# A hybrid attention and recurrence block: attention weights times values in plain float32, four gates in the second stage, an early start of the first recurrence head

## The chip, the cores and the metric

The kernel runs on one core of one Trainium2 chip. The core has a matrix engine (TensorE, PE in the profile, with its weight loads as PEld), a vector engine (DVE), a scalar engine (ACT), a general engine (POOL) and a queue that issues transfers (SP). Time is device microseconds of one execution; the number to be predicted is the median of several executions.

## The reference, cut to what matters

1024 frames and 16 learned meta tokens in front of them (1040 rows of 1024 channels) are normalised and projected to 6144 columns. Two branches read the projections: stick-breaking attention with 8 heads of 64, and a gated linear recurrence with 4 heads of 128. Both are gated, projected to 1024 channels, merged by sigmoid gates per channel, and projected once more.

```
proj = u @ w_in            # 1040 x 6144: q k v gate | hq hf hi hgate | gate_sb gate_hg
weights = where(s < t, exp(log_sigmoid(z) + later), 0)      # z = q k^T, later: sum of log(1-beta)
y_sb = (weights @ v) * silu(sb_gate)
S = diag(f) S + (1-f) i^T ;  o = S^T q                      # per recurrence head
y_hg = groupnorm(o) * silu(hg_gate)
merged = sigmoid(gate_sb) * (y_sb @ w_sb_out) + sigmoid(gate_hg) * (y_hg @ w_hg_out)
h = h + merged @ w_out ;  out = rmsnorm(h)
```

All of it is float32. The two gate matrices, gate_sb and gate_hg, have 1024 columns each, that is eight tiles of 128 columns each.

## The kernel before, in words

**Two ways to multiply.** Most products split both operands into a high part that the matrix engine takes in one pass (type F32R) and the rest, and add three products (high by high, high by rest, rest by high). Transposes, and the products inside the recurrence, take plain float32 operands; the trace shows each of these plain products as two records.

**Stages.** (1) Normalise, transpose, first projections. (2) From 67.7 us on, "twins": a projection of 256 columns and all frames is done with seven products of half size in place of eight (`product`, L466; operand preparation in `prep`, L454 on ACT and L455 on POOL). A list `twins` holds eleven of them; the last three are six gate tiles of gate_sb, `N_GS = 6`. Each twin is 7 x 12 matmuls of 512 columns. (3) Attention, from 281 us: four pairs of heads `p`, each with its own projections of v and k. (4) The recurrence, four heads, from 573 us. (5) The projections of the branches, the merge, and the output product.

**What fills the gaps.** Attention and recurrence are chains that pass between engines. Into them a list of projections is threaded: `interleave(steps, lead)` takes for each pair a `main` list of small pieces and a `fill` list, and issues fill pieces in proportion to the main work done, 4 us ahead in attention (LEAD_A) and 2 us in the recurrence (LEAD_B). Fill is the next pair's v and k projections and the gate tiles that are not in a twin: a gate tile there is `gate_group`, 2 halves of 24 matmuls of 512 columns (L259), with a weight fetch of 512 KB, a split of the weights on ACT (L115) and POOL (L120) and a sigmoid on ACT (L1001). `FILL = (2,1,1,1)` says how many gate tiles go into each attention pair, `n = (1,1,2,1)` how many into each recurrence head. What order the instructions then have on each engine is set by the framework's scheduler from this order and its own priorities.

**Attention.** The work of one head comes in units `g = 0..3`, each two blocks of 128 queries. `scores` makes products of queries and keys (L626), a sigmoid on ACT (L628) and a running product along the row on DVE (L631, L635); the result is the sticks `w` (tile `ab`). `values` turns blocks of w by transposes on PE (L668, and L650 for the 16 meta columns), copies them out of PSUM on ACT (L670) as the high part and forms the rest by a subtraction on DVE (L671), then multiplies: the value block with its 64 high and 64 rest columns is the stationary operand, w of two query blocks the moving one,

```
for part in range(2):
    for j in range(2):
        T.matmul(self.av, st["v"][hh][:, 2 * gg + j], wt[:, part, where[j]:where[j] + 256], ...)
```

(L682; four matmuls of 256 columns for each group of up to four blocks, one more for the meta tokens, L685). The sum stands transposed, channels by queries. Its two halves are added (copy on ACT, L688; sum on DVE, L689), and DVE multiplies by the gate (L693). While the values of one unit are made, the scores of the next are threaded between them (`zip_quanta`). PSUM has two buffers for transposes (`tr`), two for scores (`z`), and one for this sum (`av`).

**Recurrence.** `recurrence(hd, ...)` gives twelve pieces. The first, `diagonal`, is DVE work alone (L825 to L843): elementwise products of keys and queries, and the first products of decay factors. `quads` follows with many small matmuls (L852, L858) and DVE updates (L910, L913), then `sixteens` (L877), `halves` (L891), transposes and the state products (L929 to L970). The queries of the head are fetched into a buffer `wt`, of which there are two.

Of the kernel before, what the change touches and what calls it, by code (L numbers as in the profile page):

```python
# [8 lines left out]
F32 = mybir.dt.float32  # L9
F32R = mybir.dt.float32r  # L10
U8 = mybir.dt.uint8
AF = mybir.ActivationFunctionType
# [24 lines left out]
REAL = [(NM, 512), (NM + 512, 512)]  # L37
FULL = [(0, 348), (348, 346), (694, 346)]
QUART = [(0, 256), (256, 256), (512, 256), (768, 272)]
N_GS = 6  # L40
WS = 456
FILL = (2, 1, 1, 1)


@with_exitstack
def block_kernel(ctx: ExitStack, tc: tile.TileContext, x, meta, norm_g, w_in, w_sb_out,
# [379 lines left out]
    twins += [(C_HQ + 2 * P * k, 2 * k, out_silu(kept_hq, HG_SCALE)) for k in range(2)]  # L426
    twins += [(C_HG + 2 * P * k, 2 * k, out_silu(kept_hg, 1.0)) for k in range(2)]
    twins += [(C_GS + 2 * P * k, 2 * k, out_gate(C_GS)) for k in range(N_GS // 2)]

    def ured(c0, t0):  # L430
        return uh[:, c0:c0 + 4, t0:t0 + HT], ul[:, c0:c0 + 4, t0:t0 + HT]
# [73 lines left out]
    here.append(ctx.enter_context(phase("rest")))  # L505


    t = sb("wt", [P, 2, 2, 512], F32R)
    V.memset(t[:, :, :, 0:P].bitcast(F32), 0.0)
    wt_last = [t[:, k] for k in range(2)]  # L510
    t = sb("wt", [P, 2, 2, 512], F32R)
    wt_full = [t[:, k] for k in range(2)]
    n_full = [0]
    t = sb("wtm", [P, 2, 256], F32R)
    V.memset(t.bitcast(F32), 0.0)
    wt_meta = [t[:, k] for k in range(2)]
    t = sb("vm", [P, 2, 2, P], F32R)
    V.memset(t.bitcast(F32), 0.0)
    v_meta = [t[:, k] for k in range(2)]

    later = sb("later", [P, WS])
# [4 lines left out]
    def pair_groups(p):  # L526
        st = {}

        def bk():
            st["k"] = [sb("stk", [P, L], F32R) for _ in range(2)]  # L530
            st["y"] = sb("y", [P, SEQ])
            nc.sync.dma_start(st["y"], kept_sg[p])

        def bv():
            st["vt"] = sb("pt", [P, L + 1])
            st["dv"] = sb("pt", [P, L + 1])
            st["ve"] = sb("ve", [P, NB])
            V.memset(st["vt"][:, 0:1], 0.0)

        def ek(acc, t0, n):  # L540
            for hh in range(2):
                r0, r1 = hh * 64, 64 - hh * 64
                kst = st["k"][hh]
                src = acc[r0:r0 + 64]
                hi = kst[r0:r0 + 64, t0:t0 + n]
                S.activation(hi, src, AF.Copy)
                V.tensor_tensor(kst[r1:r1 + 64, t0:t0 + n], src, hi.bitcast(F32), op=ALU.subtract)

        def ev(acc, t0, n):

            vt = st["vt"]
            S.activation(vt[:, t0 + 1:t0 + n + 1], acc, AF.Copy)
            V.tensor_tensor(st["dv"][:, t0:t0 + n], vt[:, t0:t0 + n], acc, op=ALU.subtract)
            if t0 + n == L:
                G.tensor_copy(st["ve"], vt[:, NM + P:NM + P + (NB - 1) * P + 1:P])

        def v_blocks(b4):
            def emit():
                if b4 == 0:
                    st["v"] = [sb("v", [P, NB, P], F32R) for _ in range(2)]  # L560
                tp = ps("tr").rearrange("p (b n) -> p b n", b=4)
                for b in range(4):
                    t0 = NM + (b4 * 4 + b) * P
                    T.transpose(tp[:, b], st["dv"][:, t0:t0 + P], ident)
                for hh in range(2):
                    src = tp[:, :, hh * 64:hh * 64 + 64]
                    hi = st["v"][hh][:, b4 * 4:b4 * 4 + 4, 0:64]
                    S.activation(hi, src, AF.Copy)
                    V.tensor_tensor(st["v"][hh][:, b4 * 4:b4 * 4 + 4, 64:128], src, hi.bitcast(F32), op=ALU.subtract)
            return (440.0, emit)  # L570

        def v_meta_block():
            vm = v_meta[p % 2]
            st["vm"] = vm
            tp = ps("tr")
            T.transpose(tp[:NM, 0:P], st["dv"][:, 0:NM], ident)
            for r0 in (0, 32):
                src = tp[:NM, 0:P].rearrange("p (h n) -> p h n", h=2)
                S.activation(vm[r0:r0 + NM, :, 0:64], src, AF.Copy)
                V.tensor_tensor(vm[r0:r0 + NM, :, 64:128], src, vm[0:NM, :, 0:64].bitcast(F32), op=ALU.subtract)  # L580

        after_v = [v_blocks(0), v_blocks(1), (110.0, v_meta_block)]
        return st, [proj(C_V + P * p, FULL, ev, bv, after_v), proj(C_K + P * p, FULL, ek, bk)]

# [8 lines left out]
    class Unit:  # L593
# [46 lines left out]
        def values(self):  # L640
# [6 lines left out]
            def meta_t():  # L647
                tp = ps("tr")
                for qi in range(2):
                    T.transpose(tp[:NM, qi * P:(qi + 1) * P], self.w[qi][:, 0:NM], ident)  # L650
                wm = wt_meta[k]
                with tc.high_priority(offset=HP):
                    S.activation(wm[0:NM], tp[:NM, :256], AF.Copy)
                    V.tensor_tensor(wm[32:32 + NM], tp[:NM, :256], wm[0:NM].bitcast(F32), op=ALU.subtract)

            def bank_t(gg):
                def emit():
                    tp = ps("tr")
                    if gg < g:
                        cols = [(j, qi, (j * 2 + qi) * P) for qi in range(2) for j in range(2)]  # L660
                        wt, lo, where = wt_full[n_full[0] % 2], 0, (0, 256)
                        n_full[0] += 1
                    else:
                        cols = [(0, 0, 2 * P), (1, 1, P), (0, 1, 3 * P)]
                        wt, lo, where = wt_last[k], P, (256, 0)
                    for j, qi, c in cols:
                        s0 = NM + (2 * gg + j) * P
                        T.transpose(tp[:, c:c + P], self.w[qi][:, s0:s0 + P], ident)  # L668
                    with tc.high_priority(offset=HP):
                        S.activation(wt[:, 0, lo:], tp[:, lo:], AF.Copy)  # L670
                        V.tensor_tensor(wt[:, 1, lo:], tp[:, lo:], wt[:, 0, lo:].bitcast(F32), op=ALU.subtract)  # L671
                    wts[gg] = (wt, where)
                return (440.0, emit)

            def bank_av(gg):
                def emit():
                    if gg == g:
                        self.av = ps("av")[:, :256]
                    wt, where = wts[gg]
                    for part in range(2):  # L680
                        for j in range(2):
                            T.matmul(self.av, st["v"][hh][:, 2 * gg + j], wt[:, part, where[j]:where[j] + 256],  # L682
                                     start=(gg == g and part == 0 and j == 0), stop=False)
                    if gg == 0:
                        T.matmul(self.av, st["vm"][:, hh], wt_meta[k], start=False, stop=True)  # L685
                        av = self.av
                        tmp = sb("sg", [P, 256])
                        S.activation(tmp[0:64], av[64:128], AF.Copy)  # L688
                        V.tensor_tensor(tmp[r0:r0 + 64], av[0:64], tmp[0:64], op=ALU.add)  # L689
                        for qi in range(2):  # L690
                            b = 2 * g + qi
                            y = st["y"][r0:r0 + 64, P * b:P * (b + 1)]
                            V.scalar_tensor_tensor(y, tmp[r0:r0 + 64, qi * P:(qi + 1) * P], st["ve"][r0:r0 + 64, b:b + 1], y,  # L693
                                                   op0=ALU.add, op1=ALU.mult)
                return (440.0 + 110.0 * (gg == 0), emit)

            q.append(bank_t(g))
            if g > 0:
# [2 lines left out]
            for gg in range(g, -1, -1):  # L701
                q.append(bank_av(gg))
                if gg > 1:
                    q.append(bank_t(gg - 2))
            return q

    def zip_quanta(a, b):

# [381 lines left out]
    late_q = stream(pairs[1][1][:1], pairs[1][1][1])  # L1090
    emit_all(late_q[:CUT])
    emit_all(zip_quanta(late_q[CUT:], both(units[0], "scores")))
    rest = [gate_group(C_GS, e) for e in range(N_GS, 8)] + [gate_group(C_GH, e) for e in range(8)]
    share = FILL
    side, k0 = [], 0
    for p in range(4):
# [6 lines left out]
    for p in range(4):  # L1103
        main = []
        for i in range(6 * p, 6 * p + 6):
            main.append((0.0, lambda i=i: ahead(i + 2)))
            nxt = both(units[i + 1], "scores") if i + 1 < len(units) else []
            main += zip_quanta(both(units[i], "values"), nxt)
            if 7 <= i < 7 + len(MASKS):
                main.append((0.0, lambda h=MASKS[i - 7]: mask_after(h)))  # L1110
        steps.append((main, stream(side[p], side[p + 1][0] if p < 3 else heads[1][1][0])))
    interleave(steps, LEAD_A)

    def hg_gate(h):
# [7 lines left out]

    tail = []
    for h in range(4):
        main, t = recurrence(h, heads[h][0], ("q", "ab", "v", "ab")[h])
        main = main[:2] + tail + main[2:]
        tail = t + [hg_gate(h)]
        n = (1,1,2,1)[h]
        some, rest = rest[:n], rest[n:]
        if h < 3:  # L1130
            fill = stream(heads[h + 1][1] + some, heads[h + 2][1][0] if h < 2 else (rest + sbg)[0])
# [259 lines left out]
```

## Time and profile before

| | |
|---|---|
| median of 3 executions | 892.31 us (892.25 to 893.4) |
| the profiled execution | 892.41 us |
| its span in the profile | 890.7 us, so 1.7 us lie outside it |
| second stage (twins) | 67.7 to 281 us |
| attention, first projections | 281 to 323 us |
| attention, threaded | 323 to 573 us |
| recurrence | 573 to about 740 us |
| busy over the span | PE 868.2, DVE 626.2, ACT 410.9, POOL 280.3 us |

PE rows need care: matmuls overlap in the pipeline, so the mean duration of one is longer than the distance from one to the next. That distance (called pitch below) is read from the chain of waits, where consecutive pieces do not overlap, or from the start times of consecutive rows. Engine shares over the whole span mix stages with different limits.

### The profile page before, as it was taken

What the parts mean: (1) busy time and instruction counts of PE and PEld (TensorE: products, weight loads), DVE (VectorE), ACT (ScalarE), POOL (GpSimd) and SP (SyncE); (2) the same over time, 40 slices, a digit from 0 to 9 for tenths busy, and PEclk for the clock granted to TensorE, in tenths of its full rate; (3) what the DMA queues carried; (4) which work ended last, traced back from release to release, by engine and by line L of the source; (5) the groups of instructions that cost most, each with busy time, mean ns of one, the idle gap of its engine ahead of it and who ended that gap; (6) DMA issues with size and microseconds to landing.
All of it is one profiled execution on the core that took longest, in us unless ns stands there. A gap on an engine that the chain in (4) does not pass through costs nothing.

```text
span 890.7 us, 15024 instructions
## 1 busy us (share of the span) xinstructions
PE 868.2 (97%) x5684; PEld 750.6 (84%) x5684; DVE 626.2 (70%) x1084; ACT 410.9 (46%) x950; POOL 280.3 (31%) x303
## 2 busy tenths in 40 slices
PE   7999999999999999999999999999999999999996
PEld 5998888888888998899899898879788788888885
DVE  6894455645433378789789788867665989998875
ACT  7763334333432455556556556434435364223432
POOL 1027444544451211123211122447261100004551
PEclk9999999999999999999999999999999999999999
DMA  9223444333343512311213212212312357663212
GB/s 286 67 71 93 160 145 131 95 107 118 119 130 116 169 41 67 96 60 48 84 60 96 86 59 60 84 44 102 121 63 80 129 182 259 197 222 125 95 47 96
DMA packets 90587, 98.12 MB, mean 110 GB/s; under 512 B 6017, under 2 KB 65281, under 8 KB 90514
## 3 DMA queue, kind: packets, MB, share of 16 engines
q1 hardware_dynamic: 76832, 73.78, 27.4%
q10 hardware_dynamic: 13682, 23.37, 7.1%
q8 instruction: 45, 0.74, 0.3%
q14 instruction: 28, 0.23, 0.1%
HBM read 71.94 MB, written 25.20 MB: 109 GB/s over the span
## 4 chain that ended last, share of the span: by engine, by line
PE 84%; DVE 8%; ACT 4%; issue 1%; DMA 1%; POOL 0%; ACTq 0%; SPq 0%; DVEq 0%; POOLq 0%
PE acc L259 33%; PE acc L466 10%; PE z L466 7%; PE tr L466 7%; PE acc L1298 4%; PE av L682 3%; PE tr L668 3%; PE z L626 3%; PE z L1298 3%; PE tr L1298 3%; PE acc L350 2%; DVE ab L635 2%; DVE ab L631 1%; ACT sq L169 1%; PE av L949 1%
## 5 line engine op out<-in xcount | busy, mean ns | idle before, releaser
L259 PE MATMUL acc<-uh,wh 128*128 128x346 f32 (+2 forms) x472 | 173.4, 367 | 0.0
L120 POOL TENSOR_TENSOR wl<-wr,wh 128x256 fp32r<-128x256 f32 x92 | 79.0, 879 | 271.8 <-ACT wh L115 244.2
L259 PE MATMUL acc<-ul,wh 128*128 128x346 f32 (+2 forms) x472 | 164.2, 348 | 0.0
L259 PE MATMUL acc<-uh,wl 128*128 128x346 f32 (+2 forms) x472 | 163.8, 347 | 0.0
L259 PEld LDWEIGHTS acc<-uh,wl 128*128 128x128 f32 x472 | 88.8, 188 | 6.8
L259 PEld LDWEIGHTS acc<-uh,wh 128*128 128x128 f32 x472 | 89.0, 189 | 4.2 <-issue 0.4
L259 PEld LDWEIGHTS acc<-ul,wh 128*128 128x128 f32 x472 | 89.2, 189 | 2.9 <-issue 0.4
L455 POOL TENSOR_TENSOR pw<-su,pw 128x512 fp32r<-128x512 f32 x44 | 59.2, 1365 | 42.8 <-ACT pw L454 42.8
L455 POOL TENSOR_TENSOR pw<-wr,pw 128x512 fp32r<-128x512 f32 x33 | 43.7, 1323 | 62.5 <-ACT pw L454 62.5
L628 ACT ACTIVATE ab<-z 128x456 f32<-128x456 f32 (+6 forms) x112 | 49.8, 448 | 26.4 <-PE z L626 25.9
L631 DVE TENSOR_TENSOR_SCAN ab<-ab,later 128x456 f32<-128x456 f32 (+3 forms) x64 | 55.7, 871 | 6.8 <-ACT ab L628 6.1
L466 PE MATMUL acc<-th,pw 128*128 128x512 f32 x176 | 58.0, 390 | 0.0
L671 DVE TENSOR_TENSOR wt<-tr,wt 128x384 fp32r<-128x384 f32 (+1 forms) x80 | 50.4, 630 | 10.0 <-ACT wt L670 7.8
L670 ACT ACTIVATE wt<-tr 128x384 fp32r<-128x384 f32 (+1 forms) x80 | 44.3, 554 | 26.0 <-PE tr L668 25.8
L682 PE MATMUL av<-wt,v 128*128 128x256 f32 x320 | 52.6, 286 | 3.7 <-DVE sg L689 3.1
L626 PE MATMUL z<-stk,q 128*128 128x456 f32 (+6 forms) x224 | 55.8, 331 | 0.0
L454 ACT ACTIVATE pw<-su 128x512 fp32r<-128x512 f32 x44 | 26.0, 626 | 60.9 <-DVE su L449 27.1
L682 PEld LDWEIGHTS av<-wt,v 128*128 128x128 f32 x320 | 46.2, 188 | 8.3 <-DVE sg L689 5.3
L635 DVE TENSOR_TENSOR_SCAN ab<-ab 128x348 f32<-128x348 f32 (+4 forms) x48 | 47.0, 980 | 7.2 <-ACT ab L628 5.7
L668 PE MATMUL tr<-ident,ab 128*128 128x128 f32 x288 | 45.2, 273 | 0.7 <-DVE ab L631 0.7
L115 ACT ACTIVATE wh<-wr 128x256 fp32r<-128x256 f32 x92 | 34.4, 413 | 24.6 <-PE acc L259 15.6
L626 PEld LDWEIGHTS z<-stk,q 128*128 128x128 f32 x224 | 38.3, 189 | 3.4
(378 smaller groups left out, 2035.4 us busy)
## 6 DMA issues: line engine op xcount, KB each, us to landing
wr<-in_w_in SPq DMA_DIRECT2D x48, 512.0 KB, 4.1
q<-q SPq DMA_DIRECT2D x32, 256.0 KB, 4.2
wr<-in_w_out SPq DMA_DIRECT2D x16, 512.0 KB, 3.5
sg<-gate SPq DMA_DIRECT2D x24, 256.0 KB, 3.2
gate<-sg ACTq DMA_DIRECT2D x20, 256.0 KB, 2.0
xb<-in_x SPq DMA_DIRECT2D x7, 512.0 KB, 8.1
gate<-co ACTq DMA_DIRECT2D x12, 256.0 KB, 2.0
pt<-hi SPq DMA_DIRECT2D x4, 520.0 KB, 3.2
```

What stands on the lines that cost most here:

```text
L120: eng.tensor_tensor(lo[:, cs], raw[:, cs], h[:, cs].bitcast(F32), op=ALU.subtract)
L259: T.matmul(acc, a, b, start=(k == 0), stop=(k == total - 1))
L455: G.tensor_tensor(t[:, 1], d[key], t[:, 0].bitcast(F32), op=ALU.subtract)
L466: T.matmul(acc, t[:, part // 2, c], (bh, bl, bh)[part][:, c], start=(c == part == 0), stop=(c == 3 and part == 2))
L626: T.matmul(z, qt[:, k, qo + qi * P:qo + (qi + 1) * P], st["k"][hh][:, c0:c1], start=(k == 0), stop=(k == 1))
L628: S.activation(a[:, c0:c1], z, AF.Sigmoid, scale=-1.0)
L631: ins = V.tensor_tensor_scan(w, w, later[:, WS - (n - c0):][:, ::-1], 1.0, op0=ALU.mult, op1=ALU.max)
L635: V.tensor_tensor_scan(w, w, w, a[:, c1:c1 + 1], op0=ALU.mult, op1=ALU.bypass)
L668: T.transpose(tp[:, c:c + P], self.w[qi][:, s0:s0 + P], ident)
L671: V.tensor_tensor(wt[:, 1, lo:], tp[:, lo:], wt[:, 0, lo:].bitcast(F32), op=ALU.subtract)
L682: T.matmul(self.av, st["v"][hh][:, 2 * gg + j], wt[:, part, where[j]:where[j] + 256], start=(gg == g and part == 0 and j == 0), stop=False)
L1298: T.matmul(a, t[:, part // 2, c], (bh, bl, bh)[part][c][:, n * HT // 2:n * HT // 2 + a.shape[-1]], start=(c == part == 0), stop=(c == 3 an ...
```

## The change

1. **Sticks times values.** The transposed sticks stay one plain float32 tile; no rest is formed on DVE. They are now the stationary operand, one 128x128 block for each matmul, and 64 columns of a plain float32 value tile move. The sum stands queries by channels. One ACT copy puts it into a tile `by_query`, and when both heads of a pair have their columns there, a new piece `close` turns it back with two transposes for each unit (L697 after) and DVE applies the gate out of PSUM (L699 after). `close` of a unit is issued behind the first two pieces of the next one. The value tile is one plain copy.
2. **Gates.** `N_GS = 8`, `N_GH = 2`: two more twins, so four gate tiles leave the fill. `FILL = (0,0,0,2)`, and the recurrence has `n = (0,1,2,1)`.
3. **First head.** The `diagonal` of head 0 stands before the last piece of the last attention unit.
4. **Buffers.** The transposed sticks rotate through four buffers of tag `v`; one of the two `wt` buffers holds `by_query`, the other is free for head 0's queries from the start of attention. Memsets of padded tiles go.

```diff
-N_GS = 6
+N_GS = 8
+N_GH = 2
-FILL = (2, 1, 1, 1)
+FILL = (0, 0, 0, 2)
...
+    twins += [(C_GH + 2 * P * k, 2 * k, out_gate(C_GH)) for k in range(N_GH // 2)]
...
-    t = sb("wt", [P, 2, 2, 512], F32R)
-    V.memset(t[:, :, :, 0:P].bitcast(F32), 0.0)
-    wt_last = [t[:, k] for k in range(2)]
-    t = sb("wt", [P, 2, 2, 512], F32R)
-    wt_full = [t[:, k] for k in range(2)]
+    wt_full = []
+    for _ in range(2):
+        t = sb("v", [P, 2, 512])
+        wt_full += [t[:, k] for k in range(2)]
+    t = sb("wt", [P, 2, NB, P])
+    by_query = [t[:, k] for k in range(2)]
...
                     with tc.high_priority(offset=HP):
-                        S.activation(wt[:, 0, lo:], tp[:, lo:], AF.Copy)
-                        V.tensor_tensor(wt[:, 1, lo:], tp[:, lo:], wt[:, 0, lo:].bitcast(F32), op=ALU.subtract)
-                    wts[gg] = (wt, where)
+                        S.activation(wt[:, :n], tp[:, :n], AF.Copy)
+                    wts[gg] = (wt, cols)
...
-                    for part in range(2):
-                        for j in range(2):
-                            T.matmul(self.av, st["v"][hh][:, 2 * gg + j], wt[:, part, where[j]:where[j] + 256],
-                                     start=(gg == g and part == 0 and j == 0), stop=False)
-                    if gg == 0:
-                        T.matmul(self.av, st["vm"][:, hh], wt_meta[k], start=False, stop=True)
-                        av = self.av
-                        tmp = sb("sg", [P, 256])
-                        S.activation(tmp[0:64], av[64:128], AF.Copy)
-                        V.tensor_tensor(tmp[r0:r0 + 64], av[0:64], tmp[0:64], op=ALU.add)
...
+                    for c, (j, qi) in enumerate(cols):
+                        T.matmul(self.av[:, qi], wt[:, c * P:c * P + P], st["v"][:, 2 * gg + j, r0:r0 + 64],
+                                 start=(gg == g and c == 0), stop=False)
+                    if gg > 0:
+                        return
+                    for qi in range(2):
+                        T.matmul(self.av[:, qi], wt_meta[k][:, qi * P:(qi + 1) * P], st["vm"][:, r0:r0 + 64],
+                                 start=False, stop=(qi == 1))
+                    S.activation(st["o"][:, 2 * g:2 * g + 2, r0:r0 + 64], self.av, AF.Copy)
...
+        def close(self):
+            st, g = self.st, self.g
+            def emit():
+                tp = ps("tr")
+                for qi in range(2):
+                    b = 2 * g + qi
+                    T.transpose(tp[:, qi * P:(qi + 1) * P], st["o"][:, b], ident)
+                    y = st["y"][:, P * b:P * (b + 1)]
+                    V.scalar_tensor_tensor(y, tp[:, qi * P:(qi + 1) * P], st["ve"][:, b:b + 1], y, op0=ALU.add, op1=ALU.mult)
+            return [(220.0, emit)] if self.hh else []
...
-            main += zip_quanta(both(units[i], "values"), nxt)
+            vals = both(units[i], "values")
+            vals[2:2] = both(units[i - 1], "close") if i else []
+            main += zip_quanta(vals, nxt)
+            if i + 1 == len(units):
+                main += both(units[i], "close")
...
+    main0, tail0 = recurrence(0, heads[0][0], "q")
+    last = steps[3][0]
+    for k, quantum in zip((-1,), main0):
+        last.insert(k, quantum)
+    main0 = main0[1:]
...
-        n = (1,1,2,1)[h]
+        n = (0, 1, 2, 1)[h]
```

PE, in the last pair of heads, the values of a unit with g = 3 (tr: a transpose buffer, wt: transposed sticks, v: values, z: scores of the next unit, acc: fill). Before:

```order
L626 MATMUL z_5646<-stk_4645,q_5384 128x328 x2
L682 MATMUL av_5651<-wt_2528,v_4701 128x256 x4
L259 MATMUL acc_5642<-uh_72,wh_5167 128x512
L259 MATMUL acc_5642<-ul_73,wh_5167 128x512
L259 MATMUL acc_5642<-uh_72,wl_5168 128x512
L668 MATMUL tr_5659<-ident_63,ab_5505 128x128 x2
L668 MATMUL tr_5659<-ident_63,ab_5539 128x128 x2
L626 MATMUL z_5667<-stk_4645,q_5384 128x392 x2
L682 MATMUL av_5651<-wt_2530,v_4701 128x256 x4
```

and now, where v_2809 and v_2808 hold the transposed sticks and v_4700 the values:

```order
L620 MATMUL z_5477<-stk_4644,q_5233 128x328 x2
L669 MATMUL av_5482<-v_4700,v_2809 128x64 x3
L260 MATMUL acc_5399<-uh_72,wh_4988 128x512
L260 MATMUL acc_5399<-ul_73,wh_4988 128x512
L260 MATMUL acc_5399<-uh_72,wl_4989 128x512
L656 MATMUL tr_5492<-ident_63,ab_5349 128x128
L656 MATMUL tr_5492<-ident_63,ab_5386 128x128 x2
L656 MATMUL tr_5492<-ident_63,ab_5349 128x128
L260 MATMUL acc_5510<-uh_72,wh_5256 128x512
```

Four matmuls of 256 columns have become three or four of 64; the transposes and the fill around them keep their places.

DVE, where attention ends and head 0 of the recurrence begins. Before:

```order
L689 TENSOR_TENSOR sg_5833<-av_5823,sg_5833 64x256
L693 SCALAR_TENSOR_TENSOR y_4646<-sg_5833,ve_4394,y_4646 64x128 x2
L689 TENSOR_TENSOR sg_5844<-av_5838,sg_5844 64x256
L693 SCALAR_TENSOR_TENSOR y_4646<-sg_5844,ve_4394,y_4646 64x128 x2
L825 TENSOR_TENSOR ab_5849<-stk_5160,wt_5163 128x1024
L915 TENSOR_TENSOR ab_5853<-stk_5159 128x520
L827 TENSOR_TENSOR wt_5163<-wt_5163,stk_5159 128x1024
```

and now:

```order
L625 SCALAR_TENSOR_TENSOR ab_5606<-ab_5606,later_2813 128x144
L625 SCALAR_TENSOR_TENSOR ab_5606<-ab_5606,later_2813 128x272
L820 TENSOR_TENSOR ab_5718<-stk_4981,wt_4984 128x1024
L910 TENSOR_TENSOR ab_5722<-stk_4980 128x520
L822 TENSOR_TENSOR wt_4984<-wt_4984,stk_4980 128x1024
L910 TENSOR_TENSOR ab_5722<-ab_5722 128x260
L836 TENSOR_TENSOR wt_4984<-wt_4984,stk_4980 128x256x2
```

The diagonal (L825, now L820) stood behind the last gate products of attention; it now stands directly behind the last running products, ahead of the gate products of the last three units (L699).

PE at the same place, now (before, the first L852 stood 19 rows behind the last L685):

```order
L674 MATMUL av_5689<-vm_2812,wtm_2811 128x64 x2
L847 MATMUL z_5730<-ab_5718,o_684_4233 32x256 x4
L853 MATMUL z_5735<-wt_4984,stk_4981 32x48 x21
L669 MATMUL av_5706<-v_4700,v_2809 128x64 x3
L674 MATMUL av_5706<-vm_2812,wtm_2811 128x64 x2
L697 MATMUL tr_5713<-ident_63,wt_2810 128x128
```

The first small products of the recurrence (L847, L853) now stand between the products of the last two units, ahead of the last of them.

More of the change, by code (lines that the diff above doesn't have):

```diff
@@ L505, in block_kernel @@
     here.append(ctx.enter_context(phase("rest")))
-    t = sb("wt", [P, 2, 2, 512], F32R)
-    V.memset(t[:, :, :, 0:P].bitcast(F32), 0.0)
-    wt_last = [t[:, k] for k in range(2)]
-    t = sb("wt", [P, 2, 2, 512], F32R)
-    wt_full = [t[:, k] for k in range(2)]
+    wt_full = []
+    for _ in range(2):
+        t = sb("v", [P, 2, 512])
+        wt_full += [t[:, k] for k in range(2)]
     n_full = [0]
-    t = sb("wtm", [P, 2, 256], F32R)
-    V.memset(t.bitcast(F32), 0.0)
+    t = sb("wt", [P, 2, NB, P])
+    by_query = [t[:, k] for k in range(2)]
+    t = sb("wtm", [NM, 2, 256])
     wt_meta = [t[:, k] for k in range(2)]
-    t = sb("vm", [P, 2, 2, P], F32R)
-    V.memset(t.bitcast(F32), 0.0)
+    t = sb("vm", [NM, 2, P])
     v_meta = [t[:, k] for k in range(2)]
@@ L559, in emit @@
                 if b4 == 0:
-                    st["v"] = [sb("v", [P, NB, P], F32R) for _ in range(2)]
+                    st["v"] = sb("v", [P, NB, P])
                 tp = ps("tr").rearrange("p (b n) -> p b n", b=4)
@@ L564, in emit @@
                     T.transpose(tp[:, b], st["dv"][:, t0:t0 + P], ident)
[L565 to L569, printed above, removed]
+                S.activation(st["v"][:, b4 * 4:b4 * 4 + 4], tp, AF.Copy)
             return (440.0, emit)
         def v_meta_block():
-            vm = v_meta[p % 2]
-            st["vm"] = vm
+            st["vm"] = v_meta[p % 2]
             tp = ps("tr")
             T.transpose(tp[:NM, 0:P], st["dv"][:, 0:NM], ident)
[L577 to L580, printed above, removed]
+            S.activation(st["vm"], tp[:NM, 0:P], AF.Copy)
+        st["o"] = by_query[p % 2]
         after_v = [v_blocks(0), v_blocks(1), (110.0, v_meta_block)]
@@ L650, in meta_t @@
                     T.transpose(tp[:NM, qi * P:(qi + 1) * P], self.w[qi][:, 0:NM], ident)
-                wm = wt_meta[k]
                 with tc.high_priority(offset=HP):
-                    S.activation(wm[0:NM], tp[:NM, :256], AF.Copy)
-                    V.tensor_tensor(wm[32:32 + NM], tp[:NM, :256], wm[0:NM].bitcast(F32), op=ALU.subtract)
+                    S.activation(wt_meta[k], tp[:NM, :256], AF.Copy)
             def bank_t(gg):
@@ L658, in emit @@
                     tp = ps("tr")
[L659 to L666, printed above, removed]
+                    cols = [(0, 0), (0, 1), (1, 1)] + [(1, 0)] * (gg < g)
+                    wt = wt_full[n_full[0] % 4]
+                    n_full[0] += 1
+                    for c, (j, qi) in enumerate(cols):
                         s0 = NM + (2 * gg + j) * P
-                        T.transpose(tp[:, c:c + P], self.w[qi][:, s0:s0 + P], ident)
+                        T.transpose(tp[:, c * P:c * P + P], self.w[qi][:, s0:s0 + P], ident)
+                    n = len(cols) * P
                     with tc.high_priority(offset=HP):
-                        S.activation(wt[:, 0, lo:], tp[:, lo:], AF.Copy)
-                        V.tensor_tensor(wt[:, 1, lo:], tp[:, lo:], wt[:, 0, lo:].bitcast(F32), op=ALU.subtract)
-                    wts[gg] = (wt, where)
+                        S.activation(wt[:, :n], tp[:, :n], AF.Copy)
+                    wts[gg] = (wt, cols)
                 return (440.0, emit)
@@ L677, in emit @@
                     if gg == g:
-                        self.av = ps("av")[:, :256]
-                    wt, where = wts[gg]
-                    for part in range(2):
-                        for j in range(2):
-                            T.matmul(self.av, st["v"][hh][:, 2 * gg + j], wt[:, part, where[j]:where[j] + 256],
-                                     start=(gg == g and part == 0 and j == 0), stop=False)
-                    if gg == 0:
-                        T.matmul(self.av, st["vm"][:, hh], wt_meta[k], start=False, stop=True)
-                        av = self.av
-                        tmp = sb("sg", [P, 256])
[L688 to L695, printed above, removed]
+                        self.av = ps("av")[:, :P].rearrange("p (q n) -> p q n", q=2)
+                    wt, cols = wts[gg]
+                    for c, (j, qi) in enumerate(cols):
+                        T.matmul(self.av[:, qi], wt[:, c * P:c * P + P], st["v"][:, 2 * gg + j, r0:r0 + 64],
[6 more added lines that the diff above has]
+                    S.activation(st["o"][:, 2 * g:2 * g + 2, r0:r0 + 64], self.av, AF.Copy)
+                return (440.0 + 220.0 * (gg == 0), emit)
             q.append(bank_t(g))
@@ L1092, in block_kernel @@
     emit_all(zip_quanta(late_q[CUT:], both(units[0], "scores")))
-    rest = [gate_group(C_GS, e) for e in range(N_GS, 8)] + [gate_group(C_GH, e) for e in range(8)]
+    rest = [gate_group(C_GS, e) for e in range(N_GS, 8)] + [gate_group(C_GH, e) for e in range(N_GH, 8)]
     share = FILL
@@ L1124, in block_kernel @@
     for h in range(4):
-        main, t = recurrence(h, heads[h][0], ("q", "ab", "v", "ab")[h])
+        main, t = recurrence(h, heads[h][0], (None, "ab", "v", "ab")[h]) if h else (main0, tail0)
         main = main[:2] + tail + main[2:]
         tail = t + [hg_gate(h)]
-        n = (1,1,2,1)[h]
+        n = (0, 1, 2, 1)[h]
         some, rest = rest[:n], rest[n:]
```

## The prediction

> **What bounds the kernel now.** I read the page first, then busy time by stage, then the chain of waits for the distances between instructions, then the waits.
>
> ```profile
> span 890.7 us, 15024 instructions
> PE 868.2 (97%) x5684; PEld 750.6 (84%) x5684; DVE 626.2 (70%) x1084; ACT 410.9 (46%) x950; POOL 280.3 (31%) x303
> PE 84%; DVE 8%; ACT 4%; issue 1%; DMA 1%; POOL 0%; ACTq 0%; SPq 0%; DVEq 0%; POOLq 0%
> ```
>
> PE is busy for 97% and holds 84% of the chain that ended last. By stage (start:end, length, busy time of each engine):
>
> ```profile
> 67.70:281.00 213.30, 213.30 (x931) 174.35 (x931) 101.79 (x149) 78.00 (x137) 103.28 (x80) 1.00 0.38 121
> 323.00:390.00 67.00, 66.34 (x425) 59.70 (x424) 53.55 (x90) 37.72 (x90) 12.00 (x12) 1.00 0.25 76
> 520.00:573.00 53.00, 51.43 (x346) 46.22 (x345) 44.15 (x79) 31.38 (x76) 11.07 (x12) 1.00 0.21 61
> 323.00:573.00 250.00, 245.20 (x1618) 224.53 (x1617) 205.17 (x353) 143.79 (x350) 53.48 (x73) 1.00 0.24 72
> 573.00:612.00 39.00, 37.90 (x513) 32.30 (x512) 28.82 (x55) 14.91 (x48) 20.50 (x18) 1.00 0.29 95
> ```
>
> The columns behind the length are PE, PEld, DVE, ACT, POOL. In the second stage PE never rests. In threaded attention it is idle for 250 - 245.2 = 4.8 us, in head 0 of the recurrence for 1.1 us. So PE time taken out anywhere after 67.7 us shortens the kernel nearly one for one, as long as the other engines keep up; DVE is the next, 205 of 250 us in attention and 83% (44.15 of 53) in its last quarter, which has least fill and most idle PE (1.57 us).
>
> **The gates.** The chain gives the pitch of both kinds of projection:
>
> ```profile
> 757.93 42.08 PE acc L259 x180
> 84.39 5.55 PE acc L466 x24
> 103.71 5.55 PE acc L466 x24
> ```
>
> 42.08/180 = 0.2338 us for a 512-column matmul; a gate tile in the fill is 48 of them, 11.2 us, four are 44.9 us. The same place of one twin and the next is 103.71 - 84.39 = 19.32 us apart, so two more twins cost 38.6 us. Out of attention go three tiles (five, now two), out of the recurrence one (five, now four). PE: 38.6 - 44.9 = **-6.2 us**. The twins' operand preparation on POOL fills 103 of 213 us and stays covered by PE; without that cover two twins would cost 18.8 us of POOL work, less than their 38.6.
>
> **Sticks times values on PE.** The old form and the nearest plain float32 rows:
>
> ```profile
> 567.08 0.47 PE av L682 x4
> L682 PE MATMUL av<-wt,v 128*128 128x256 f32 x320 | 52.6, 286 | 3.7 <-DVE sg L689 3.1 <-DVE wt L671 0.3
> L685 PE MATMUL av<-wtm,vm 128*128 128x256 f32 x32 | 9.1, 284 | 0.0
> L668 PE MATMUL tr<-ident,ab 128*128 128x128 f32 x288 | 45.2, 273 | 0.7 <-DVE ab L631 0.7
> 602.13 0.94 PE av L949 x8
> 617.97 0.44 PE tr L991 x4
> 43.70 0.66 PE L189 MATMUL tr<-ident,xb 16*128 16x16 f32 x8
> 594.82 0.61 PE z L891 x16
> ```
>
> Before: 0.47/4 = 0.1175 us, times 320 + 32, is 41.4 us. After: 288 blocks (as many as transposes, L668) and 32 x 2 meta products, each plain, so two records each as in L949 and L891: 704 records. No row has 128 weight columns and 64 moving ones. L949 moves 128 columns in at most 0.94/8 = 0.118 us a record; by the L991 pitch, 0.11, half of it is 0.055, the lower end. L189 loads 128 weight columns of 16 rows and moves 16: 0.66/8 = 0.083 with the pipeline's tail, and with a tail of about 0.2 us taken off (an estimate from L682's mean of 286 against its pitch of 118) near 0.062. L891 loads 64 columns of all 128 rows and moves 64: two records make 128 weight columns in 2 x 0.61/16 = 0.076, which I take as the upper end. I choose 0.062: the row that has the same number of weight columns. 704 x 0.062 = 43.6, so **+2.3 us** (from -2.7 to +12.1).
>
> A rule speaks against this. The Trainium skill, TensorE: Matmul & The Clock Gate, section "LDWEIGHTS (loading the stationary operand)", gives a load as the number of columns divided by 1.2, in ns: about 107 ns for 128 columns, however few move. By it the sum would be 704 x 0.107 = 75.3 us; the L189 row, 8 loads in 0.66 us, does not agree with it.
>
> **Turning back.** `close` adds 4 x 4 x 2 = 32 transposes of 0.11 us: **+3.5 us** of PE. PE in all: -6.2 + 2.3 + 3.5 = -0.4.
>
> **DVE and ACT in attention.** What goes, and what stays on the path of a unit:
>
> ```profile
> L671 DVE TENSOR_TENSOR wt<-tr,wt 128x512 fp32r<-128x512 f32 x48 | 32.8, 684 | 8.0 <-ACT wt L670 7.0
> L671 DVE TENSOR_TENSOR wt<-tr,wt 128x384 fp32r<-128x384 f32 x32 | 17.6, 550 | 1.9 <-ACT wt L670 0.8
> L670 ACT ACTIVATE wt<-tr 128x512 fp32r<-128x512 f32 x48 | 28.7, 598 | 16.8 <-PE tr L668 16.8
> L693 DVE SCALAR_TENSOR_TENSOR y<-sg,ve,y 64x128 f32<-64x128 f32 x64 | 20.1, 353 | 1.0
> L689 DVE TENSOR_TENSOR sg<-av,sg 64x256 f32<-64x256 f32 x32 | 13.3, 415 | 17.9 <-ACT sg L688 17.6
> L654 DVE TENSOR_TENSOR wtm<-tr,wtm 16x256 fp32r<-16x256 f32 x32 | 13.3, 414 | 2.3 <-ACT wtm L653 1.4
> L688 ACT ACTIVATE sg<-av 64x256 f32<-64x256 f32 x32 | 12.2, 381 | 38.6 <-PE av L685 38.4
> ```
>
> DVE loses 32.8 + 17.6 + 13.3 + 13.3 us and half of L693 (32 instructions of the same 128 columns): 87 of 205 us. ACT keeps its copies. The first quarter, which keeps no gate tile, becomes 67 - 22.4 + 1.4 = 46 us of PE (two tiles out, a quarter of 2.3 + 3.5 in) with ACT at 37.72 less the tiles' own sigmoids and splits (an estimate: some 5.7), 32, and DVE at 53.55 - 22 = 32: both at 70%. That is no worse than DVE's 83% in today's last quarter, so I expect no new bound. The named waits:
>
> ```profile
> PE av L682 <- DVE sg L689: 3.1, 5, 0.9
> PE tr L668 <- DVE ab L631: 0.7, 1, 0.7
> PE z L877 <- DVE wt L913: 2.3, 2, 1.6
> PE z L858 <- DVE wt L843: 1.4, 2, 1.0
> ```
>
> The one `av` buffer is released today by copy and sum (0.381 + 0.415 us, the sum queued on DVE); afterwards by one copy. With the lighter DVE I take **-3 us** of these 3.8 in attention. What is late next is the copy of the transposed sticks on ACT (0.598), which the load of the stationary operand now waits for. From both sides: -4.1 (every named wait, L671's 0.3 with them) to +11 (below).
>
> **First head.** Its start on DVE:
>
> ```profile
> 573.04 1.23 DVE L825 TENSOR_TENSOR ab<-stk,wt 128x1024 f32<-128x1024 f32 x1
> 579.38 0.69 DVE L910 TENSOR_TENSOR stk<-stk,stk 128x520 f32<-128x520 f32 x1
> 584.09 0.92 PE z L858 x61
> ```
>
> From 573.04 to 579.38 DVE works off the diagonal and what belongs to it. In the new order that stands under the last two units, whose DVE has room. The fetch of head 0's queries stands far ahead on the SP queue, with a free buffer. Without that cover the 6.3 us return and nothing is won. PE only loses 1.1 us in this window, and half of the 3.7 us of waits at L858 and L877 are head 0's: **-1 us** (0 to -2.5). Against it, head 0 loses 11.2 us of fill: 37.9 - 11.2 = 26.7 us of PE over 28.82 us of DVE, less 6.3 now done earlier, leave 22.5. DVE is under PE, but the chain has little slack: **+1 us** (0 to +4).
>
> **Sum**, on the profiled execution's 892.41 us (span 890.7 and 1.7 around it; the median shown is 892.31, the same to 0.1): -6.2 + 2.3 + 3.5 - 3 - 1 + 1 = -3.4, so **889.0 us**.
>
> **The rivals.** (B) *Waits vanish and weights load at the lower end.* 704 x 0.055 makes -2.7 in place of +2.3, attention gives -4.1, head 0's two terms -1.1: -6.2 - 2.7 + 3.5 - 4.1 - 1.1 = -10.6, 881.8 us. For it: DVE drops by 87 us. Against: no row shows 0.055 with 128 weight columns.
>
> (C) *The missing fill bares the ACT copy.* In the first three quarters three gate tiles, 33.7 us of PE, leave 18 unit steps. A product then stands behind its own transposes with little between; where less PE work lies between than one copy and one more ACT instruction in front of it, about 1.1 us, PE waits. One bare copy of 0.598 in each of 18 steps is +10.8: 889.0 + 10.8 = 899.8, slower. For it: ACT ends most idle time of its neighbours (the releasers of L671, L689). Against: ACT has 30% room, and the DVE step behind that copy is gone.
>
> (D) *Weights set the pace.* If a record costs what plain 128-column rows cost, 0.11, 704 of them make 77.4 us in place of 43.6: 922.8 us. Against it stands the L189 row. The skill's rule above would give nearly this, 920.7 us.
>
> (E) *`close` blocks the transposes.* It holds one of two `tr` buffers until DVE has done two gate products (0.353 each); if each of 16 closes delays the next block by one of them, +5.6: 894.6 us. It decides where the DVE queue has running products in front.
>
> **How the numbers follow.** A measurement of this kernel tells about 0.2% from no change, 1.8 us: faster is below 890.5, slower above 894.1. The forecast's own range is 885 to 893, chance 0.48 (0.34 faster, 0.13 the same, 0.01 slower). B 0.20, faster. E 0.12 (0.05 the same, 0.07 slower). C 0.15 and D 0.05, slower. Faster 0.54, same 0.18, slower 0.28. The range leaves out D, the far half of C and a little of B: 881 to 900.
>
> **What would show it.** The second stage ends near 320 us (281 + 38.6), PE without a gap. The chain's pitch of the new products (av, two records each) near 0.062: 0.055 speaks for B, 0.11 for D. PE idle in threaded attention under 4.8 us and no wait on `av` for DVE; waits of the av loads for the ACT copy of transposed sticks, most in the first quarter, mean C; waits of transposes for the gate products of `close` mean E. The first L858 products of the recurrence inside attention's last 3 us. I am wrong if attention's stage, less its fill, grows by more than 5 us, or if the twins' pitch changes.

## The result and the profile after

The changed kernel takes 934.21 us (933.88 to 935.89) against 892.41 us of the kernel before on the same chip: a ratio of 1.047, 95% interval 1.0452 to 1.0488. It is slower by 42 us. Its profiled execution has a span of 932.5 us, 41.8 us more than before.

The page's first lines and its chain by engine, after:

```profile
span 932.5 us, 15597 instructions
PE 912.9 (98%) x6044; PEld 792.7 (85%) x6044; DVE 541.9 (58%) x903; ACT 411.0 (44%) x938; POOL 272.9 (29%) x301
PE 88%; ACT 4%; DVE 3%; issue 2%; POOL 1%; DMA 1%; ACTq 0%; SPq 0%; DVEq 0%; POOLq 0%
```

DVE lost 84 us of work (626.2 to 541.9), as forecast. PE gained 45 us, and PE holds more of the chain than before. So the time was not lost to waiting: PE has more to do. By stage (length, then PE, PEld, DVE, ACT, POOL):

```profile
67.70:320.00 252.30, 252.30 (x1101) 206.18 (x1101) 115.17 (x172) 92.22 (x163) 125.77 (x103) 1.00 0.37 119
363.00:621.33 258.33, 255.95 (x1868) 238.19 (x1866) 120.01 (x172) 132.06 (x322) 32.12 (x41) 0.99 0.19 54
```

The second stage grew from 213 to 252 us, PE without a gap, as the two twins were priced. Threaded attention (it ends at 621.33 us, with the last meta product) is where the account fails. Three gate tiles of 11.2 us left it, so of the 245.2 us of PE before 211.5 should remain, and PE is busy for 256.0 of 258.3 us; its idle time there halved, from 4.8 to 2.4 us. Something in attention costs PE over 40 us more. The chain of waits in one stretch of it, after, tells what (av is the sum of sticks times values, L669 its block products, L674 its meta products, acc the fill):

```profile
370.89 0.11 PE av L674
371.00 0.35 PE acc L260
...
372.05 0.48 PE acc L260 x3
...
373.67 0.61 PE av L669 x6
374.29 0.53 PE acc L260 x3
...
375.70 0.84 PE av L669 x8
376.54 0.53 PE acc L260 x3
377.07 0.84 PE av L669 x8
377.91 0.58 PE av L674 x4
```

Six records (two for each product) take 0.61 us, eight 0.84. If the first of a run takes 0.055 us and each further one 0.112, the runs come to 0.055 + 5 x 0.112 = 0.615 and 0.055 + 7 x 0.112 = 0.839: that fits both. A record with a longer instruction in front of it runs at the pace of its 64 moving columns, every other one at twice that. What the first record saves, the instruction behind the run pays back: the three fill products take 0.53 us there, and 0.48 behind other work (372.05). Four meta records take 0.58 us, 0.13 more than 4 x 0.112. In all: 576/8 x 0.84 = 60.5 us and 32 x 0.58 = 18.6 us, 79 us where 43.6 was predicted and 41.4 stood before.

### The profile page after: what moved, and what is told of

It reads as the page before. It is cut to its first block, busy times and chain, and to the rows that moved or that the text cites. A ratio compares the mean times of both kernels' runs of the same rounds, so it can differ in the third digit from the quotient of the medians.

```text
span 932.5 us, 15597 instructions
## 1 busy us (share of the span) xinstructions
PE 912.9 (98%) x6044; PEld 792.7 (85%) x6044; DVE 541.9 (58%) x903; ACT 411.0 (44%) x938; POOL 272.9 (29%) x301
## 4 chain that ended last, share of the span: by engine, by line
PE 88%; ACT 4%; DVE 3%; issue 2%; POOL 1%; DMA 1%; ACTq 0%; SPq 0%; DVEq 0%; POOLq 0%
PE acc L260 30%; PE acc L468 12%; PE z L468 8%; PE tr L468 8%; PE av L669 6%; PE acc L1302 3%; PE z L620 3%; PE tr L656 3%; PE z L1302 3%; PE tr L1302 2%; PE acc L351 2%; PE av L674 2%; PE tr L644 1%; ACT sq L170 1%; DVE ab L625 1%
## 5 line engine op out<-in xcount | busy, mean ns | idle before, releaser
L260 PE MATMUL acc<-uh,wh 128*128 128x346 f32 (+2 forms) x408 | 153.0, 375 | 0.0
L260 PE MATMUL acc<-ul,wh 128*128 128x346 f32 (+2 forms) x408 | 139.4, 342 | 0.0
L260 PE MATMUL acc<-uh,wl 128*128 128x346 f32 (+2 forms) x408 | 138.8, 340 | 0.0
L121 POOL TENSOR_TENSOR wl<-wr,wh 128x256 fp32r<-128x256 f32 x76 | 58.6, 792 | 228.2 <-ACT wh L116 200.1
L260 PEld LDWEIGHTS acc<-uh,wh 128*128 128x128 f32 x408 | 77.1, 189 | 5.8 <-issue 0.8
L669 PEld LDWEIGHTS av<-v,v 128*128 128x128 f32 x576 | 72.9, 191 | 0.6
L669 PE MATMUL av<-v,v 128*128 128x64 f32 x576 | 72.6, 268 | 0.0
L659 ACT ACTIVATE v<-tr 128x384 f32<-128x384 f32 (+1 forms) x80 | 44.0, 556 | 35.3 <-PE tr L656 34.0
L468 PEld LDWEIGHTS acc<-th,pw 128*128 128x128 f32 x208 | 39.0, 188 | 8.5
L468 PE MATMUL acc<-tl,pw 128*128 128x512 f32 x104 | 40.7, 391 | 0.0
## 6 DMA issues: line engine op xcount, KB each, us to landing
q<-q SPq DMA_DIRECT2D x32, 256.0 KB, 3.9
sg<-gate SPq DMA_DIRECT2D x24, 256.0 KB, 3.6
gate<-co ACTq DMA_DIRECT2D x20, 256.0 KB, 2.5
gate<-sg ACTq DMA_DIRECT2D x12, 256.0 KB, 2.0
```

Source lines behind the costliest of these rows:

```text
L121: eng.tensor_tensor(lo[:, cs], raw[:, cs], h[:, cs].bitcast(F32), op=ALU.subtract)
L260: T.matmul(acc, a, b, start=(k == 0), stop=(k == total - 1))
L468: T.matmul(acc, t[:, part // 2, c], (bh, bl, bh)[part][:, c], start=(c == part == 0), stop=(c == 3 and part == 2))
L659: S.activation(wt[:, :n], tp[:, :n], AF.Copy)
L669: T.matmul(self.av[:, qi], wt[:, c * P:c * P + P], st["v"][:, 2 * gg + j, r0:r0 + 64], start=(gg == g and c == 0), stop=False)
```

## The experiments

The first theory, "load": loading 128 plain float32 weight columns takes 0.112 us, and a stream of 64 columns (0.055 us) cannot hide the load of the next record. The rivals: the lost fill bares waits ("cover"), the 64 columns themselves take 0.112 us ("stream"), and the early start of the recurrence disturbs the order.

**The change without its gates.**

```diff
-N_GS = 8
-N_GH = 2
-FILL = (0, 0, 0, 2)
+N_GS = 6
+N_GH = 0
+FILL = (2, 1, 1, 1)
...
-        n = (0, 1, 2, 1)[h]
+        n = (1, 1, 2, 1)[h]
```

> The change without its gates: six gate tiles in twins and all fill as before, so attention has its cover back; the plain float32 products, the turning back and the early diagonal stay. Theory 'load': each record of a plain float32 product with 128 weight columns costs 0.112 us, because its weight load takes that long and the 64-column stream of 0.055 us cannot hide it. Fill changes nothing in that; only the 6 us that the twins saved come back: 940 us, records still 0.112. Theory 'cover': the loss is PE waiting in the quarters that lost their fill; with the fill back the time returns to 889 + 6 = 895 us or less.

Measured: 940.01 us, ratio 1.0528 (1.0512 to 1.0544). With all the old cover back the time rises by 5.8 us, the 6.2 us of the twins. The chain of waits in its first quarter shows the same records:

```profile
332.56 0.84 PE av L669 x8
334.40 0.84 PE av L669 x8
335.24 0.58 PE av L674 x4
```

"Cover" falls as the cause. The products, their turning back and the early start carry the whole loss.

**Meta tiles of 128 rows.**

```diff
-    t = sb("wtm", [NM, 2, 256])
+    t = sb("wtm", [P, 2, 256])
+    V.memset(t, 0.0)
...
-    t = sb("vm", [NM, 2, P])
+    t = sb("vm", [P, 2, P])
+    V.memset(t, 0.0)
```

> The change with the meta tiles (16 rows) filled up to 128 rows with zeros, as they stood before the change. In the changed kernel the first 16-row record of each unit came 0.248 us after its predecessor in place of 0.112, and the first full-height matmul behind the group came about 0.197 us late. Theory 'height': the array's change from 128 rows to 16 and back costs 0.136 + 0.197 us, 32 times: 10.7 us go, 934 becomes 923 to 924. Rival: these delays are waits for the ACT copy of the meta sticks; then nothing changes but two memsets, 934.

Measured: 925.61 us, ratio 1.0367 (1.0352 to 1.0383): 8.6 us of the expected 10.7. PE's instructions in order of time at the end of the first unit, the change first, then this kernel (start, length to the end of the last):

```profile
376.91 1.00 PE L669 MATMUL av<-v,v 128*128 128x64 f32 x8
377.84 0.65 PE L674 MATMUL av<-vm,wtm 16*128 16x64 f32 x4
378.42 0.55 PE L656 MATMUL tr<-ident,ab 128*128 128x128 f32 x3
```

```profile
376.22 1.00 PE L671 MATMUL av<-v,v 128*128 128x64 f32 x8
377.06 0.61 PE L676 MATMUL av<-vm,wtm 128*128 128x64 f32 x4
377.50 0.50 PE L658 MATMUL tr<-ident,ab 128*128 128x128 f32 x3
```

From the first product to the transposes it is 1.51 us with 16 rows and 1.28 us with 128, for the same records: 0.23 us a unit, 7.4 us for 32 units, most of the 8.6. The expected 10.7 counted the whole delay behind the meta products as a cost of the rows, but 0.05 us of it stands behind every run of these products. The shorter contraction is the slower one here. The rival, waits for the ACT copy, falls, since that copy is the same in both.

**128 moving columns.**

```diff
-                        T.matmul(self.av[:, qi], wt[:, c * P:c * P + P], st["v"][:, 2 * gg + j, r0:r0 + 64],
+                        T.matmul(self.av[:, qi], wt[:, c * P:c * P + P], st["v"][:, 2 * gg + j],
```

(with `av` and the meta products twice as wide, and the copy taking the 64 columns wanted)

> The change with 128 moving columns (the values of both heads) in each product of sticks and values, of which 64 are used; loads, records and everything behind stay. Theory 'load': a stream of 128 plain columns takes 0.112 us, as long as the load, so only the records that had their load hidden behind something longer (73 at 0.055 to 0.060) rise to 0.112: plus 4 us, 938. Theory 'stream' (the 64 columns themselves take 0.112 us): every record doubles, 704 x 0.112 = 79 us more, 1013.

Measured: 936.79 us, ratio 1.0496 (1.048 to 1.0511): 2.6 us more than the change for twice the moving columns. Its chain:

```profile
374.02 0.67 PE av L669 x6
374.69 0.47 PE acc L260 x3
376.06 0.89 PE av L669 x8
377.42 0.89 PE av L669 x8
```

0.67/6 = 0.112 and 0.89/8 = 0.111: now the first record takes as long as the rest, and the rest are unchanged. The time rose by less than the expected 4 us, since the fill behind a run is no longer late (0.47 us in place of 0.53). "Stream" falls. What paces the others is not what moves.

**One pass.**

```diff
-        t = sb("v", [P, 2, 512])
+        t = sb("v", [P, 2, 512], F32R)
...
-                    st["v"] = sb("v", [P, NB, P])
+                    st["v"] = sb("v", [P, NB, P], F32R)
```

(both meta tiles likewise)

> The change with the transposed sticks, the values and both meta tiles in the one-pass type F32R (high part only, the rest is left out, so the product is less exact): 352 records in place of 704, same columns and rows. Theory 'load' for every type: 352 x 0.112 = 39.4 us in place of 79, 934 - 40 = 894 to 896. If only the plain float32 load is slow and the one-pass load keeps to 0.062 us or less: 352 x 0.062 = 22, 934 - 57 = 877.

Measured: 893.0 us, ratio 1.0007 (0.9998 to 1.0017). Half the records cost about half, 41 us less:

```profile
371.75 0.25 PE av L669 x3
373.51 0.36 PE av L669 x4
374.43 0.36 PE av L669 x4
374.80 0.33 PE av L674 x2
```

The step from three to four records, 0.36 - 0.25, is 0.11 us again. So 128 weight columns cost 0.11 us in the one-pass type too.

**The row that misled me, as a plain product.** The prediction had its 0.062 from eight small transposes.

```diff
-            T.transpose(tp[:, c, :rows], xbs[b][:rows, ...], ident[:rows, :rows])
+            T.matmul(tp[:, c, :rows], xbs[b][:rows, ...], ident[:rows, :rows], start=True, stop=True)
```

(for the last, 16-row block alone)

> The change with the eight small transposes of the last, 16-row frame block (L189 before, 0.062 us apart) made as plain float32 products with the same identity: same 16 rows, 128 weight columns, 16 moving columns, two records each. Theory 'transposes load faster': the plain records come 0.112 us apart, like those of the changed attention. Rival 'few rows or few moving columns load faster': they come 0.062 us apart. The time as a whole moves by at most 1 to 2 us, 934 to 936.

Measured: 935.41 us in one execution. The chain of waits here, and then the row of the change for the same eight products:

```profile
44.11 1.88 PE tr L193 x16
```

```profile
43.87 0.66 PE L190 MATMUL tr<-ident,xb 16*128 16x16 f32 x8
```

1.88/16 = 0.1175 us with the first record's start in it, so 0.112 for the rest, against 0.062 as transposes: same operands, same 128 weight columns, same 16 rows and 16 moving columns. Neither few rows nor few moving columns make the load faster; the transposing form does. The weight loads of the same eight operations (PEld), in the change and here, say it directly:

```profile
L190 PEld LDWEIGHTS tr<-ident,xb 16*128 16x128 f32 x8 | 0.6, 136 | 0.1
L193 PEld LDWEIGHTS tr<-ident,xb 16*128 16x128 f32 x16 | 1.9, 186 | 0.1
```

A load is 0.050 us longer as a product, and so is the distance from record to record. The profile before held this sign, in rows that the prediction does not read, the old products and the transposes of the sticks:

```profile
L682 PEld LDWEIGHTS av<-wt,v 128*128 128x128 f32 x320 | 46.2, 188 | 8.3 <-DVE sg L689 5.3 <-DVE wt L671 0.9 <-ACT wt L670 0.2
L668 PEld LDWEIGHTS tr<-ident,ab 128*128 128x128 f32 x288 | 35.4, 140 | 5.3 <-DVE ab L631 0.9 <-DVE wt L671 0.4
```

A rival that no run here tests is a fixed price of each record, whatever it loads. Against it speaks L858, with 64 records of 32 weight columns in 0.68 us, 0.011 each (the chain before, from 610.90 us on).

**The gates alone, in the kernel before.**

```diff
-N_GS = 6
+N_GS = 8
+N_GH = 2
-FILL = (2, 1, 1, 1)
+FILL = (0, 0, 0, 2)
...
+    twins += [(C_GH + 2 * P * k, 2 * k, out_gate(C_GH)) for k in range(N_GH // 2)]
...
-        n = (1,1,2,1)[h]
+        n = (0, 1, 2, 1)[h]
```

> The kernel before with the gates alone: eight tiles of gate_sb and two of gate_hg in twins, fill (0,0,0,2) and (0,1,2,1), old products of sticks and values, no early diagonal. On PE the twins give 6.2 us: 886 us if everything else keeps up. But attention keeps its DVE load of 205 us while its PE work falls from 245 to 212 us; if PE then waits for DVE, what is won is eaten up: 890 to 896 us.

> The same four tiles in twins, but the six left spread as (1,1,1,0) over attention and (1,0,1,1) over the recurrence, so attention loses two tiles in place of three. If DVE in attention is what eats the gain, this one is ahead of the other filling: 886 to 889 us. If the fill has no part in it, both are equal.

Measured: 907.84 us (ratio 1.0174, 1.0159 to 1.0189) and 906.57 us (1.016, 1.0144 to 1.0175). Both far outside what I had expected. Threaded attention of the first, with its waits:

```profile
363.00:595.00 232.00, 217.19 (x1473) 197.86 (x1473) 202.48 (x352) 137.43 (x331) 43.46 (x62) 1.00 0.22 63
```

```profile
PE av L684 <- DVE sg L691: 4.0, 6, 0.8
PE tr L652 <- DVE wt L673: 3.5, 9, 0.6
PE av L684 <- DVE wt L673: 2.7, 5, 1.2
PE tr L670 <- DVE wt L673: 1.5, 3, 0.6
```

PE is idle for 14.8 of 232 us where it had been idle for 4.8 of 250, and DVE is busy for 87%. The longest waits are for the forming of the rests (L673) and the closing sums (L691): what the change takes away. In the other filling attention waits for the same two lines, and the recurrence waits as well: the longest wait is 5.9 us of PE for DVE at its quads. So the 6.2 us that the twins save on PE are not had beside the old DVE load.

**High part of the sticks only.** In the old form the values stay the stationary operand and 256 columns move.

```diff
-                        V.tensor_tensor(wt[:, 1, lo:], tp[:, lo:], wt[:, 0, lo:].bitcast(F32), op=ALU.subtract)
...
-                    for part in range(2):
+                    for part in range(1):
```

(the same subtraction for the meta columns, L654 before, goes too; the first and the third run also have the gates of the run above)

> The gates alone and the old form of the products, with the high part of the transposed sticks only: their rest is neither formed on DVE nor multiplied, the values keep both parts; less exact. PE loses 160 matmuls of 0.1175 us, 18.8 us, and DVE 64 us. Against the gates alone 19 us less, 868 to 872 us, if PE sets the time; the value blocks stay the stationary operand, so their loads hide behind 256 moving columns of 0.1175 us, just longer than a load of 0.112.

> The kernel before, with its six gate tiles in twins and its fill, and the high part of the transposed sticks only (their rest is neither formed nor multiplied; less exact). PE loses 18.8 us, DVE 64. If PE sets the time, 892.5 - 18.8 = 874, and less any wait for DVE in attention, 870 to 874. Against the same with four more tiles in twins (877.3) this tells what the gates are worth once DVE is light: 6 us would put it at 883, nothing or a loss at 877 or below.

> Gates in twins and high sticks only, the six tiles left spread as (1,1,1,0) over attention and (1,1,1,0) over the recurrence in place of (0,0,0,2) and (0,1,2,1). If cover in head 0 and the first quarters is what is missing in the 877.3 us, some of the 9 to 10 us by which PE waits there come back: 868 to 874 us. If the last head then runs bare, nothing is won: 876 to 880.

Measured, all less exact than the change and the kernel before:

| | us | ratio to before, interval |
|---|---|---|
| four more tiles in twins, fill as in the change | 877.27 | 0.9826 (0.9806 to 0.9846) |
| gates and fill as before | 872.68 | 0.9772 (0.9758 to 0.9785) |
| four more tiles in twins, fill moved forward | 887.04 | 0.9935 (0.9922 to 0.9947) |

The second, the kernel before without the rest of the sticks, is the fastest of all that ran: 20.2 us off, 18.8 of it the 160 matmuls of 0.1175 us, as expected. The four tiles, moved into twins, make this slower by 4.6 us, though DVE is light: the cover they gave is worth more than the 6.2 us that they save. Of these 10.8 us, 5.3 are PE's idle time in attention (7.5 us against 2.3 in the second run); where the rest lies is not shown. The 877 us missed my 868 to 872 because I had reckoned from a kernel with gates alone at about 890; it stands at 907.8. The third missed too, for the worse. Its last head and the branch projections run bare (two stretches of it, 50 and 60 us, and then the same places of the first run):

```profile
680.00:730.00 50.00, 44.16 (x444) 34.42 (x443) 44.37 (x93) 22.92 (x68) 4.79 (x5) 0.93 0.31 103
745.00:805.00 60.00, 54.71 (x231) 42.62 (x230) 52.08 (x110) 18.60 (x39) 0.99 (x1) 1.00 0.62 203
```

```profile
670.00:720.00 50.00, 48.07 (x476) 38.41 (x476) 43.47 (x90) 25.58 (x75) 5.14 (x5) 1.00 0.45 146
735.00:795.00 60.00, 59.14 (x254) 47.19 (x252) 53.34 (x113) 19.01 (x39) 1.14 (x1) 1.00 0.62 198
```

PE is idle there for 5.8 and 5.3 us, with DVE at 89% and 87%, against 1.9 and 0.9 us in the first run: 8.3 of the 9.8 us between the two. The granted clock of the first stretch is also lower, 0.93 against 1.00. I had expected "nothing is won" from a bare last head, not 10 us.

**The diagonal back in its place.**

```diff
-    for k, quantum in zip((-1,), main0):
-        last.insert(k, quantum)
-    main0 = main0[1:]
```

> The change with the diagonal of head 0 back at the start of the recurrence; everything else stays. The prediction put its early start at 1 us (0 to 2.5): 935 to 936.5 us. If the early start were one of the causes of the loss, this is faster than the change's 934.2.

Measured: 934.78 us (932.64 to 936.49), ratio 1.0469 (1.0451 to 1.0486). The change itself has 1.047 (1.0452 to 1.0488). The early start is worth nothing that five executions can tell, and is no cause of the loss.

## Why the prediction was wrong

The forecast was 889.0 us, 881 to 900, faster with a chance of 0.54. Point by point:

- **What bounds the kernel: right.** PE time counts nearly one for one. That is why a wrong price on PE came out whole.
- **The gates, -6.2 us: right in size, in part by luck.** The second stage grew by 39 us, and putting the tiles back cost 5.8 us. What I had not seen is that the gain hangs on what else fills attention: alone, the gates cost 15 us, with the high sticks 4.6. The change has over 40 us of PE work in attention that I had not forecast, and these may stand in as cover. Whether the gates would have gained 6 us had the products cost 43.6 us was not run.
- **Sticks times values on PE, +2.3 us: this step failed.** "I choose 0.062: the row that has the same number of weight columns." The row was one of transposes, and a transpose loads its weights faster than a product, as the run with the same operands as a plain product shows (0.062 against 0.112). Measured over 704 records it is 79 us, so the term is +37.6. The upper end that I had kept, 0.076, was no bound either: it came from L891, whose records load 64 columns each and write in turn to two halves of the output partitions, which is another thing than one load of 128. The rows at 0.11 (L949, L991) move as many columns as they load, so they could not tell the two prices apart.
- **What I left out: the 16 rows.** The old meta tiles were filled up to 128 rows with zeros, the new ones are not. That costs 8.6 us; nothing in the prediction speaks of it. About half of it (32 x 0.13 = 4.2 us) is in the 79.
- **Turning back, +3.5 us: right, but not all.** The transposes of `close` wait for earlier gate products, one by one, rival E's mechanism at a smaller price. The waits of PE and of its weight loads, after:

```profile
PE tr L697 <- DVE y L699: 2.0, 6, 0.6
PEld tr L697 <- DVE y L699: 4.2, 9, 0.8
```

- **Waits in attention, -3 us: about right.** No wait for DVE at `av` is left, and PE's idle time in the stage fell by 2.4 us.
- **First head, 0 in sum: not told apart.** The early start that I put at -1 us shows nothing within its executions (932.64 to 936.49). The +1 us for the fill that left has no run of its own.

The sum with the measured prices: 889.0, plus 35.5 for the products (79.1 in place of 43.6), plus 4.4 for the half of the rows' cost not in them, plus 2.0 to 4.2 for the waits of `close`, is 930.9 to 933.1; 934.2 was measured, so 1 to 3 us remain. What the runs of products hold up behind them is of that size: 44 runs in the trace have something other than meta products behind them, and at 0.53 in place of 0.48 us that makes 2.2.

Of the rivals, D ("weights set the pace", 922.8 us) had the mechanism and almost the price of a record, and I gave it 0.05. I let one row outvote it. C, the bare ACT copy, is out: attention with all its fill back is no faster. The rule that I set aside, the Trainium skill's page TensorE: Matmul & The Clock Gate, section "LDWEIGHTS (loading the stationary operand)", columns divided by 1.2 in ns, by estimate 107 ns for 128 columns, agrees with the measured 0.112 us. The same page says in its section "Terms" that weight loads and matmuls have a transpose mode, 4 times faster for FP32; it would have told me that a transpose is no witness for a product. Here a record takes 0.062 in place of 0.112 us, 1.8 times faster, and a transpose is one record where a product is two, 3.6 times faster.

## What to carry to other kernels

A matrix product in this kernel has two prices, the columns that move and the weight columns that load, and a run of them goes at the larger: a small moving side does not make a product cheap. Which operand stands still decides it, so keep as stationary the one that serves the most moving columns (256 columns hid a load of 0.112 us, 64 did not). Price a new form from a row of the same kind of instruction, or keep the range open to the dearest row of that kind. And price cover by what else is in the stage: taking four tiles of it away lost 15 us with the old DVE load, lost 4.6 with a light one, and gained 5.8 only where PE had over 40 us of other work more.

## What the runs showed of the hardware that I had not expected

- A plain product with 128 weight columns and a short stream costs 0.112 us a record here, whether 16, 64 or 128 columns move and whether 16 or 128 rows are contracted; a one-pass product with 64 moving columns costs 0.11, and the transposing form (16 rows, 16 moving columns) 0.062 us.
- Going from 128 rows to 16 and back costs about 0.23 us each time (8.6/32 = 0.27 by the time of the whole kernel); filling up with zeros is cheaper than the short contraction.
- In the first record of a run the load is hidden by the longer instruction in front, and the record takes 0.055 us; but the load of the instruction behind the run is then bare for as long, 0.53 in place of 0.48 us. So nothing here says that records set singly between long matmuls would be cheaper. That was not tried.
